# Moving 32 weight subtractions from VectorE to GpSimd in a two-layer diffusion trunk

## Chip, cores and metric

The kernel runs on one core of one Trainium2 chip. The metric is the device time of one execution in microseconds (us); the median of three runs stands for a kernel.

## What is computed

The reference passes 384 tokens (128 context tokens, 256 latent ones; model width 1024) through two layers. Each layer is a half-step SwiGLU FFN, a mixer of four head groups with one input and one output projection, and a second half-step FFN. Every sub-layer has an RMS norm, shift, scale and gate from a modulation vector, and a residual add. All data is fp32.

```
h = rms_norm(x, g) * (1 + scale) + shift
x = x + 0.5 * gate * ((silu(h @ wg) * (h @ wu)) @ wd)          # FFN, width 2816
x = x + gate * (concat(four mixers of (h @ w_in)) @ w_out)     # mixer
```

## The kernel before

Activations are kept transposed: x is eight tiles x[k] of 128 features by 384 tokens. Every large product is made of three fp32r matmuls (`mm3`, L203 to L207): a weight is split into a high part (a ScalarE copy to fp32r, L196) and a low part (weight minus high part, L197, on VectorE), an activation likewise, and high*high (L205), high*low (L206) and low*high (L207) are added up in PSUM. `weights` loads a piece of weights by a DMA of the SP queue into a "raw" buffer (5 of them) and splits it into a "hi" buffer (5) and a "lo" buffer (4). A lo buffer is free again when the matmuls that read it are done.

An FFN (`ffn`) runs over 22 blocks of 128 hidden features, in two halves of 11. A block f loads a gate piece (z = 0) and an up piece (z = 1), 128x1024 each, and makes 24 matmuls into a PSUM bank g and 24 into a bank u. The "d" banks are two, so g of block f+1 waits until g of block f has been read. The first four blocks ("early") work on x scaled but not yet normalised (hh and hl, L259 and L260, 386 columns) so that they can begin before the norm factor rstd is known. Their results are multiplied by rstd afterwards (g at L267, u at L312), and `hidden` (L287 to L290) makes the normalised inputs of the later blocks meanwhile. After each half come eight down blocks (dn).

The output projection (in `dense`, L477 to L490) runs in two passes (ph) over eight output blocks j; a pass adds four of the eight mixer tiles. Each block has a 128x512 piece of weights, twelve matmuls, and then `add_x` (L273), which reads the bank and updates x[j]. In the second pass, `nxt(j)` makes hh and hl of x[j] for the next FFN, and `ssq.add(j)` adds the squares of x[j]: for j = 1 to 6 this add is on GpSimd, for j = 7 on VectorE (L234). rstd is worked out from that sum, by a matmul with ones (L240) and two activations.

VectorE also makes part of the modulation vectors of later sub-layers between these (L170, "junk"). Which instructions an engine runs is written in the code; in which order each engine's queue holds them is settled when the kernel is built, by a scheduler that goes by program order, by when operands and buffers come free, and by its own durations. On the chip each engine's queue runs in order.

Of the kernel before, what the change touches and what calls it, by code (L numbers as in the profile page):

```python
# [11 lines left out]
ALU = mybir.AluOpType  # L12
# [4 lines left out]
D = 1024  # L17
# [26 lines left out]
def trunk(ctx, tc, a):  # L44
    nc = tc.nc
    V, S, G, PE = nc.vector, nc.scalar, nc.gpsimd, nc.tensor
# [7 lines left out]
    def nm(s):  # L54
        cnt[0] += 1
        return f"{s}_{cnt[0]}"


    def dbank(s):
        return ps.tile([P, 512], F32, tag="d", name=nm(s), bufs=2)  # L60
# [14 lines left out]
    def slot(grp, s, *shapes, dt=F32):  # L75

        t, o, out = sb.tile([P, WIDTH[grp]], dt, tag=grp, name=nm(s), bufs=NSLOT[grp]), 0, []
        for sh in shapes:
            n = int(np.prod(sh))
            v = t[:, o:o + n]  # L80
            if len(sh) == 2:
                v = v.rearrange("p (a b) -> p a b", a=sh[0])
            elif len(sh) == 3:
                v = v.rearrange("p (a b c) -> p a b c", a=sh[0], b=sh[1])
            out.append(v)
            o += n
        assert o <= WIDTH[grp], (s, o)
        return out if len(out) > 1 else out[0]

    def one(s, dt=F32):  # L90
        return sb.tile([P, T], dt, tag="one", name=nm(s), bufs=4)

    def tiny(grp, s, n):
        return sb.tile([P, 8], F32, tag="tiny" + grp, name=nm(s), bufs=7)[:, :n]
# [22 lines left out]
    def load_w(src, s):  # L117
        t = sb.tile([P, 1024], F32, tag="raw", name=nm("raw" + s), bufs=5)
        n = src.shape[-1]
        nc.sync.dma_start(out=t[:, :n], in_=src)  # L120
        return t[:, :n]
# [67 lines left out]
        return gt  # L189


    def split_w(raw, s):
        n = raw.shape[-1]
        hi = sb.tile([P, 1024], F32R, tag="hi", name=nm("hi" + s), bufs=5)[:, :n]
        lo = sb.tile([P, 1024], F32R, tag="lo", name=nm("lo" + s), bufs=4)[:, :n]
        S.activation(hi, raw, AF.Copy)  # L196
        V.tensor_tensor(lo, raw, hi, op=ALU.subtract)  # L197
        return hi, lo

    def weights(src, s):  # L200
        return split_w(load_w(src, s), s)

    def mm3(out, w, o, x, first, last):  # L203
        wh, wl = w[0][:, o:o + P], w[1][:, o:o + P]
        PE.matmul(out, wh, x[0], start=first, stop=False)  # L205
        PE.matmul(out, wh, x[1], start=False, stop=False)  # L206
        PE.matmul(out, wl, x[0], start=False, stop=last)  # L207

    def split_act(src, hi, lo):
        S.activation(hi, src, AF.Copy)  # L210
        V.tensor_tensor(lo, src, hi, op=ALU.subtract)
# [33 lines left out]
    def log_exp():  # L245
        tc.keep_in_program_order(S.preload_act_table_set(LOGEXP))
# [29 lines left out]
    def ffn(l, i, rstd, ab, nxt, side, hook=None):  # L276

        side = side()
        gt = None
        ssq = Sumsq(int(l == NL - 1 and i == 1))  # L280
        h = [None] * KD

        def hidden(k):
            t, xr = slot("M", "h", (2, T), dt=F32R), one("xr")
            at, bt = ab
            for g, cs in GROUPS:
                V.scalar_tensor_tensor(xr[:, cs], x[k][:, cs], at[:, k, g:g + 1], rstd[:, cs],  # L287
                                       op0=ALU.mult, op1=ALU.mult)
                S.activation(t[:, 0, cs], xr[:, cs], AF.Identity, bias=bt[:, k, g:g + 1])
                V.scalar_tensor_tensor(t[:, 1, cs], xr[:, cs], bt[:, k, g:g + 1], t[:, 0, cs],  # L290
                                       op0=ALU.add, op1=ALU.subtract)
            h[k] = (t[:, 0, :], t[:, 1, :])

        for half in range(2):
            act = []
            for fi in range(HF):
                f = half * HF + fi
                w = [weights(a["w_gu"][l, i, f, :, z * D:(z + 1) * D], "gu") for z in range(2)]
                bg, bu = dbank("g"), dbank("u")
                early = f < 4  # L300
                order = [(z, k) for z in range(2) for k in range(KD)]
                if f == 0:
                    order.sort(key=lambda zk: zk[1])
                for z, k in order:
                    mm3((bg, bu)[z][:, :NX if early else T], w[z], k * P,
                        (hh[:, k, :], hl[:, k, :]) if early else h[k], k == 0, k == KD - 1)
                g, u = one("g"), one("u")
                if early:
                    sh = tiny("s", "sh", 2)
                    normed(g, bg, rstd, AF.Silu)  # L310
                    V.tensor_copy(sh, bu[:, T:NX])
                    V.tensor_tensor(u, bu[:, :T], rstd, op=ALU.mult)  # L312
                    for q, cs in GROUPS:
                        V.scalar_tensor_tensor(u[:, cs], u[:, cs], sh[:, q:q + 1], g[:, cs], op0=ALU.add, op1=ALU.mult)
                    for k in range(f * KD // 4, (f + 1) * KD // 4):
                        hidden(k)
                else:
                    S.activation(g, bg[:, :T], AF.Silu)  # L318
                    V.tensor_tensor(u, g, bu[:, :T], op=ALU.mult)
                if fi % 2 == 0:  # L320
                    ah = slot("H", "ah", (2, T), dt=F32R)
                    al = slot("H", "al", (2, T), dt=F32R)
                act.append((ah[:, fi % 2, :], al[:, fi % 2, :]))
                split_act(u, *act[-1])
                if f == NF - 1:
                    log_exp()
                if hook and f == 2:
                    hook()
                side()
            if gt is None:  # L330
                gt = gate(l, 2 * i)
            for j in range(KD):
                b = dbank("dn")
                fi = 0
                for z, n in ((0, 6), (1, 5)):
                    src = a["w_dn"][l, i, half, j]
                    w = weights(src[:, :6 * P] if z == 0 else src[:, 6 * P:], "dn")
                    for o in range(n):
                        mm3(b[:, :T], w, o * P, act[fi], fi == 0, fi == HF - 1)
                        fi += 1  # L340
                add_x(j, b, gt)
                if half == 1:
                    nxt(j)
                    ssq.add(j)
                side()
        return ssq
# [71 lines left out]
    def mixers(l, rstd, gt, ab, nxt):  # L418
# [46 lines left out]
        def dense():  # L465
            for n, (name, c) in enumerate(HALVES):
                b = dbank("in")
                if (name, c) == KR:
                    narrow(b)
                else:  # L470
                    w = weights(a["w_in"][l, WIDE.index((name, c))], "in")
                    for k in range(KD):
                        mm3(b[:, :NX], w, k * P, (hh[:, k, :], hl[:, k, :]), k == 0, k == KD - 1)
                take[name](c, b)
                yield 4.0 if n < 6 else 1.5 if (name, c) == KR else 6.84
            done["in"] = True
            for ph, ks in enumerate(OUT_PARTS):  # L477
                for jj in range(4):
                    for z in range(2):
                        j = 2 * jj + z  # L480
                        w = weights(a["w_out"][l, ph, jj, :, z * 512:(z + 1) * 512], "out")
                        b = dbank("out")
                        for n, k in enumerate(ks):
                            yield from wait(("mix", k))
                            mm3(b[:, :T], w, n * P, mix[k], n == 0, n == 3)
                        add_x(j, b, gt)
                        if ph == 1:
                            nxt(j)
                            ssq.add(j)
                        yield 2.6  # L490
# [486 lines left out]
    def side(units):  # L977

        places = [[] for _ in range(NF + 2 * KD)]
        for by, l, n, p0, p1 in units:  # L980
            g = (ada_pe if by == "PE" else ada_dve)(l, n)
            for k in range(KD):
                places[p0 + k * (p1 + 1 - p0) // KD].append(g)
            if by == "PE":
                places[p1 + 1].append(g)
        first = min([NF] + [u[3] for u in units if u[0] == "DVE"])
        places[max(first - 2, 0)].insert(0, requests_of())
        todo = iter(places)

        def f():  # L990
            for g in next(todo):
                next(g)
        return f
# [179 lines left out]
```

## Time and profile before

| what | value |
|---|---|
| median of 3 runs (lowest to highest) | 1554.87 us (1551.93 to 1558.4) |
| the profiled execution's own time | 1555.26 us |
| its span, first to last instruction | 1553.5 us |
| TensorE busy, share of the span | 1510.0 us, 97% |
| VectorE busy | 1177.9 us, 76% |
| ScalarE busy | 749.1 us, 48% |
| GpSimd busy | 99.1 us, 6% |
| granted TensorE clock, mean | 0.998 |

Shares are means over stages with different limits: TensorE is nearly always busy, VectorE has stretches in which it is full and others in which it waits. In rows of the trace, DVE is VectorE, ACT is ScalarE, POOL is GpSimd, PE is TensorE, and L260 is line 260 of the kernel.

### The profile page before, as it was taken

What the parts mean: (1) busy time and instruction counts of PE and PEld (TensorE: products, weight loads), DVE (VectorE), ACT (ScalarE), POOL (GpSimd) and SP (SyncE); (2) the same over time, 40 slices, a digit from 0 to 9 for tenths busy, and PEclk for the clock granted to TensorE, in tenths of its full rate; (3) what the DMA queues carried; (4) which work ended last, traced back from release to release, by engine and by line L of the source; (5) the groups of instructions that cost most, each with busy time, mean ns of one, the idle gap of its engine ahead of it and who ended that gap; (6) DMA issues with size and microseconds to landing.
All of it is one profiled execution on the core that took longest, in us unless ns stands there. A gap on an engine that the chain in (4) does not pass through costs nothing.

```text
span 1553.5 us, 26681 instructions
## 1 busy us (share of the span) xinstructions
PE 1510.0 (97%) x10108; PEld 1422.1 (92%) x10108; DVE 1177.9 (76%) x2649; ACT 749.1 (48%) x1330; POOL 99.1 (6%) x122
## 2 busy tenths in 40 slices
PE   6999999999999999999999999999999999999997
PEld 2999999998778999999999999999877799999997
DVE  3879998969956997997987799786797599544433
ACT  4632233457788743233454323345677874333332
POOL 1000000100130100000000000001014010000001
PEclk9999999999999999999999999999999999999999
DMA  9776775652133555765654577555211145544331
GB/s 346 252 235 206 242 236 201 190 183 83 36 94 119 160 190 183 244 230 175 203 175 150 177 233 236 183 172 173 85 65 46 66 154 182 159 143 140 120 102 60
DMA packets 84464, 257.31 MB, mean 166 GB/s; under 512 B 11120, under 2 KB 14416, under 8 KB 84080
## 3 DMA queue, kind: packets, MB, share of 16 engines
q1 hardware_dynamic: 83184, 254.14, 49.9%
q8 instruction: 79, 1.29, 0.3%
q0 software_dynamic: 1152, 1.48, 0.3%
q14 instruction: 49, 0.40, 0.1%
HBM read 252.53 MB, written 2.26 MB: 164 GB/s over the span
## 4 chain that ended last, share of the span: by engine, by line
PE 66%; DVE 19%; DMA 8%; issue 4%; ACT 3%; SPq 0%; DVEq 0%; ACTq 0%
DVE junk L170 6%; PE u L205 6%; PE u L207 6%; PE u L206 6%; PE g L205 6%; PE g L207 6%; PE g L206 6%; PE dn L206 5%; PE dn L205 5%; PE dn L207 5%; DMA rawada<-in_w_adaT 4%; DVE logu L197 3%; PE in L206 3%; PE in L207 3%; PE in L205 3%
## 5 line engine op out<-in xcount | busy, mean ns | idle before, releaser
L170 DVE SCALAR_TENSOR_TENSOR junk<-rawada,req 128x512 f32<-128x512 f32 x480 | 339.1, 706 | 40.0 <-DMA rawada<-in_w_adaT 30.2
L196 ACT ACTIVATE higu<-rawgu 128x1024 fp32r<-128x1024 f32 x176 | 186.2, 1060 | 295.6 <-DMA rawgu<-in_w_gu 91.2
L197 DVE TENSOR_TENSOR logu<-rawgu,higu 128x1024 fp32r<-128x1024 f32 x176 | 214.5, 1222 | 35.6 <-PE g L207 19.8
L205 PE MATMUL dn<-ah,hidn 128*128 128x384 f32 x704 | 236.8, 336 | 0.0
L207 PE MATMUL dn<-ah,lodn 128*128 128x384 f32 x704 | 236.6, 336 | 0.0
L206 PE MATMUL dn<-al,hidn 128*128 128x384 f32 x704 | 236.6, 336 | 0.0
L196 ACT ACTIVATE hidn<-rawdn 128x768 fp32r<-128x768 f32 (+1 forms) x128 | 101.5, 793 | 254.5 <-PE dn L206 71.7
L205 PE MATMUL u<-h,higu 128*128 128x384 f32 x576 | 194.0, 337 | 3.1 <-DVE x L273 2.5
L205 PE MATMUL g<-h,higu 128*128 128x384 f32 x576 | 194.4, 338 | 1.8 <-ACT g L318 1.6
L206 PE MATMUL g<-h,higu 128*128 128x384 f32 x576 | 193.7, 336 | 0.0
L207 PE MATMUL u<-h,logu 128*128 128x384 f32 x576 | 193.6, 336 | 0.0
L207 PE MATMUL g<-h,logu 128*128 128x384 f32 x576 | 193.6, 336 | 0.0
L206 PE MATMUL u<-h,higu 128*128 128x384 f32 x576 | 193.6, 336 | 0.0
L197 DVE TENSOR_TENSOR lodn<-rawdn,hidn 128x768 fp32r<-128x768 f32 (+1 forms) x128 | 113.2, 885 | 30.1 <-issue 17.0
L205 PEld LDWEIGHTS dn<-ah,hidn 128*128 128x128 f32 x704 | 132.3, 188 | 0.4 <-issue 0.3
L206 PEld LDWEIGHTS dn<-al,hidn 128*128 128x128 f32 x704 | 132.4, 188 | 0.0
L207 PEld LDWEIGHTS dn<-ah,lodn 128*128 128x128 f32 x704 | 132.3, 188 | 0.0
L234 POOL TENSOR_TENSOR ssq<-ssq,sq 128x384 f32<-128x384 f32 x42 | 46.9, 1117 | 1160.5 <-DVE hl L260 752.7
L205 PEld LDWEIGHTS g<-h,higu 128*128 128x128 f32 x576 | 108.3, 188 | 5.0 <-ACT g L318 2.4
L205 PEld LDWEIGHTS u<-h,higu 128*128 128x128 f32 x576 | 108.3, 188 | 4.3 <-issue 3.1
L206 PEld LDWEIGHTS g<-h,higu 128*128 128x128 f32 x576 | 108.3, 188 | 0.2 <-DVE h L290 0.2
L206 PEld LDWEIGHTS u<-h,higu 128*128 128x128 f32 x576 | 108.3, 188 | 0.0
(297 smaller groups left out, 2844.9 us busy)
## 6 DMA issues: line engine op xcount, KB each, us to landing
rawgu<-in_w_gu SPq DMA_DIRECT2D x176, 512.0 KB, 4.2
rawada<-in_w_adaT SPq DMA_DIRECT2D x120, 512.0 KB, 3.7
rawdn<-in_w_dn SPq DMA_DIRECT2D x64, 384.0 KB, 3.3
rawdn<-in_w_dn SPq DMA_DIRECT2D x64, 320.0 KB, 3.0
rawin<-in_w_in SPq DMA_DIRECT2D x38, 512.0 KB, 3.7
rawada<-in_w_ada SPq DMA_DIRECT2D x24, 512.0 KB, 6.2
rawout<-in_w_out SPq DMA_DIRECT2D x32, 256.0 KB, 2.7
req<-in_c SPq DMA_DIRECT2D x16, 256.0 KB, 4.0
```

Of the source, the lines that this page charges most:

```text
L170: V.scalar_tensor_tensor(xbank("junk")[:, 0, :], t[:, z * 512:(z + 1) * 512], 1.0, requests[v, z], op0=ALU.mult, op1=ALU.mult, accum_out=s ...
L196: S.activation(hi, raw, AF.Copy)
L197: V.tensor_tensor(lo, raw, hi, op=ALU.subtract)
L205: PE.matmul(out, wh, x[0], start=first, stop=False)
L206: PE.matmul(out, wh, x[1], start=False, stop=False)
L207: PE.matmul(out, wl, x[0], start=False, stop=last)
L234: (V if self.n == KD - 1 else G).tensor_tensor(self.acc, self.acc, sq, op=ALU.add)
```

## The change

`split_w` and `weights` get an argument `low`, the engine of the subtraction at L197. It is GpSimd (G) for the up piece of blocks 0 to 3 of each FFN (4 pieces of 128x1024 in each of 4 FFNs, 16 in all) and for all pieces of the output projection's second pass (8 pieces of 128x512 in each of 2 layers, 16 in all). The other low parts stay on VectorE.

```diff
-    def split_w(raw, s):
+    def split_w(raw, s, low=None):
...
         S.activation(hi, raw, AF.Copy)
-        V.tensor_tensor(lo, raw, hi, op=ALU.subtract)
+        (low or V).tensor_tensor(lo, raw, hi, op=ALU.subtract)
         return hi, lo
-    def weights(src, s):
-        return split_w(load_w(src, s), s)
+    def weights(src, s, low=None):
+        return split_w(load_w(src, s), s, low)
...
-                w = [weights(a["w_gu"][l, i, f, :, z * D:(z + 1) * D], "gu") for z in range(2)]
+                w = [weights(a["w_gu"][l, i, f, :, z * D:(z + 1) * D], "gu", G if f < 4 and z == 1 else None)
+                     for z in range(2)]
...
-                        w = weights(a["w_out"][l, ph, jj, :, z * 512:(z + 1) * 512], "out")
+                        w = weights(a["w_out"][l, ph, jj, :, z * 512:(z + 1) * 512], "out", G if ph == 1 else None)
```

## Rows read from the trace of the kernel before

**Rows 1.** The page's first part: busy us (share of span) xinstructions per engine.

```profile
PE 1510.0 (97%) x10108; PEld 1422.1 (92%) x10108; DVE 1177.9 (76%) x2649; ACT 749.1 (48%) x1330; POOL 99.1 (6%) x122
```

**Rows 2.** Waits of PE, whole span: us in total, times, longest us.

```profile
PE ada L145 <- DMA rawada<-in_w_ada: 13.3, 15, 5.6
...
PE u L205 <- ACT hh L259: 1.4, 1, 1.4
...
PE g L205 <- DVE g L267: 1.1, 3, 0.5
...
PE u L205 <- ACT higu L196: 0.4, 1, 0.4
```

**Rows 3.** Timeline of PE, 508 to 528 us: start, us, instruction, [idle before <-releaser].

```profile
510.13 0.34 PE L207 MATMUL out<-mix,loout 128*128 128x384 f32 x1
510.78 0.41 PE L205 MATMUL out<-mix,hiout 128*128 128x384 f32 x1 [0.31 <-ACT hh L259]
...
514.00 0.41 PE L205 MATMUL g<-hh,higu 128*128 128x386 f32 x1 [0.88 <-ACT hh L259]
...
517.20 0.42 PE L205 MATMUL u<-hh,higu 128*128 128x386 f32 x1 [0.49 <-DVE x L273]
...
524.40 0.41 PE L205 MATMUL g<-hh,higu 128*128 128x386 f32 x1 [0.29 <-DVE g L267]
```

**Rows 4.** Timeline of DVE, 495 to 580 us.

```profile
499.29 0.74 DVE L260 SCALAR_TENSOR_TENSOR hl<-x,A,hh 128x128 fp32r<-128x128 f32 x2
...
504.27 0.74 DVE L273 SCALAR_TENSOR_TENSOR x<-out,G,x 128x128 f32<-128x128 f32 x2
...
507.00 1.55 DVE L197 TENSOR_TENSOR logu<-rawgu,higu 128x1024 fp32r<-128x1024 f32 x1
508.48 1.50 DVE L260 SCALAR_TENSOR_TENSOR hl<-x,A,hh 128x128 fp32r<-128x128 f32 x2
...
518.77 0.54 DVE L234 TENSOR_TENSOR ssq<-ssq,sq 128x384 f32<-128x384 f32 x1
```

**Rows 5.** Timeline of POOL, whole span.

```profile
19.66 1.00 POOL L234 TENSOR_TENSOR ssq<-ssq,sq 128x384 f32<-128x384 f32 x1 [19.21 <-ACT sq L232]
...
429.49 0.86 POOL L889 TENSOR_TENSOR d<-dh 128x406 f32<-128x406 f32 x1 [7.51 <-DVE sc L383]
...
504.03 1.05 POOL L234 TENSOR_TENSOR ssq<-ssq,sq 128x384 f32<-128x384 f32 x1 [1.04 <-ACT sq L232]
...
508.53 1.18 POOL L234 TENSOR_TENSOR ssq<-ssq,sq 128x384 f32<-128x384 f32 x1 [1.05 <-ACT sq L232]
```

**Rows 6.** DVE groups by form, 498.03 to 519.31 us: xcount | busy us, mean ns.

```profile
L260 DVE SCALAR_TENSOR_TENSOR hl<-x,A,hh 128x256 fp32r<-128x256 f32 x8 | 6.1, 764 | 0.0
L197 DVE TENSOR_TENSOR logu<-rawgu,higu 128x1024 fp32r<-128x1024 f32 x4 | 5.2, 1294 | 0.0
...
L197 DVE TENSOR_TENSOR loout<-rawout,hiout 128x512 fp32r<-128x512 f32 x4 | 2.8, 688 | 0.0
L260 DVE SCALAR_TENSOR_TENSOR hl<-x,A,hh 128x128 fp32r<-128x128 f32 x8 | 2.7, 341 | 0.0
```

**Rows 7.** Three stretches: length; busy us of PE, PEld, DVE, ACT, POOL; clock, DMA, GB/s.

```profile
498.03:519.31 21.28, 19.59 (x110) 18.72 (x109) 21.01 (x42) 17.76 (x33) 6.63 (x6) 1.00 0.62 200
788.97:797.43 8.46, 7.09 (x41) 6.80 (x40) 8.46 (x14) 4.65 (x8) 1.17 (x1) 1.00 0.76 237
524.16:549.87 25.71, 25.47 (x144) 25.50 (x145) 25.59 (x63) 15.84 (x31) 0.00 (x0) 1.00 0.42 134
```

**Rows 8.** Timeline of DVE, 780 to 812 us.

```profile
794.45 0.73 DVE L273 SCALAR_TENSOR_TENSOR x<-dn,G,x 128x128 f32<-128x128 f32 x2
...
803.15 0.16 DVE L266 COPY sh<-g 128x2 f32<-128x2 f32 x1 [5.71 <-PE g L207]
```

**Rows 9.** DVE and PE in the timeline, 529 to 533 us.

```profile
529.87 0.55 DVE L267 TENSOR_TENSOR g<-g,rstd 128x384 f32<-128x384 f32 x1
...
532.98 0.34 PE L205 MATMUL g<-hh,higu 128*128 128x386 f32 x1
```

## The prediction

> **What bounds the kernel now.** I read the page's busy times first. TensorE is busy 1510.0 of 1553.5 us, 97% [rows 1]: work that is taken off another engine gives at most the time that TensorE now waits for that engine. So the second view is TensorE's waits. The largest item, 13.3 us for the first modulation weights, is a load at the start that the change does not touch [rows 2]. What it could touch stands in the third view, the timeline of TensorE at the end of the first mixer: it idles 0.31, 0.88 and 0.49 us while banks come free, and 0.29 us before the g matmuls of block 1 of the next FFN, whose bank waits for the normalisation at L267 [rows 3]. Together that is 2.0 us. Here VectorE is the reason: in the 21.28 us that end there it is busy 21.01 [rows 7].
>
> The fourth view, VectorE's timeline set beside GpSimd's, decides the case. A pair of L260 instructions takes 0.74 us when GpSimd rests, but the pair that begins at 508.48 takes 1.50 [rows 4]. GpSimd ran a 128x384 add from 508.53 to 509.71 [rows 5]. The pair ends at 508.48 + 1.50 = 509.98, 0.27 after the add: its second instruction stood until the add was over. The subtraction at 507.00 takes 1.55 in the same way. L273, however, takes its plain 0.74 from 504.27 to 505.01 [rows 4], wholly inside the GpSimd add of 504.03 to 505.08 [rows 5]. L260 and L197 read two tensors from SBUF, L273 reads one from PSUM and one from SBUF. I read this as: an instruction of VectorE with two SBUF inputs and a two-input instruction of GpSimd do not run at the same time; one with a PSUM input is free. It goes both ways, since the GpSimd add takes 1.00 undisturbed and 1.18 when it meets VectorE [rows 5].
>
> **A rule of the Trainium skill on this.** The page "SBUF — State Buffer", section "Who interferes with whom", says more than these rows: that the lock is held for the whole instruction, whatever its length. The rows agree for adds of 1.2 us; no run here shows a longer one. If GpSimd let VectorE in halfway through a longer one, the excess below would be about half; by the rule it is whole.
>
> From the rows alone, where the bar lasts to the end of the add, I take the whole duration.
>
> **The price of a subtraction on GpSimd.** No row shows a 128x1024 or 128x512 subtraction there, nor one that writes fp32r. The nearest rows are the two-tile add of 384 columns in 1.00 us, 2.6 ns a column, and an add of one tile with itself shifted, 406 columns in 0.86, 2.1 ns a column [rows 5]. That gives 2.17 to 2.67 us for 1024 columns and 1.08 to 1.33 for 512. I take 2.6 and 1.3, near the two-tile add, since the subtraction reads two tiles too. On VectorE the same work costs 1.21 (the mean of 1.294 over four, with the blocked one of 1.55 taken out: (4 x 1.294 - 1.55)/3) and 0.69 [rows 4, 6]. So each moved piece frees VectorE of 1.21 or 0.69 us and bars its two-input instructions for 2.6 or 1.3.
>
> The Trainium skill has another price: "GPSIMD Engine Reference", section 3.1, gives 4497 ns for an add of 2048 columns, from which I estimate 2.25 us for 1024 columns and 1.12 for 512. No run here shows it. The sum below would come to about 8 us by it instead of 11.
>
> **Mixer ends, twice (once per layer).** From 498.03 to 519.31 I add up all that excludes each other: L260 eight pairs of 0.74 = 5.9; L197 4 x 1.21 + 4 x 0.69 = 7.6; the last square sum on VectorE 0.5 [rows 4]; GpSimd's adds 6.63 [rows 7]. The sum is 20.6 of 21.28: about 0.7 free. The change takes out four out pieces and two up pieces (blocks 0 and 1), 4 x 0.69 + 2 x 1.21 = 5.2, and adds 4 x 1.3 + 2 x 2.6 = 10.4. The excess is 10.4 - 5.2 - 0.7 = 4.5 us; with the low prices 2.8 (4 x 1.08 + 2 x 2.17 = 8.7), with the high ones 4.8. The other four out pieces fall before 498, where lo buffers are ready several blocks ahead; I cost them at nothing, hidden by TensorE's matmuls. The 4.5 reaches TensorE nearly whole, as it already waits there for this very chain: L273 stands behind L260 in VectorE's queue, the banks behind L273, and L267 behind the square sum and rstd [rows 3]. GpSimd's adds for j = 1 to 6 queue behind the subtractions as well, and the last add behind them. Twice 4.5 is 9.0 us (5.6 to 9.6).
>
> **Start of layer 1's first FFN.** From 788.97 to 797.43 VectorE is busy throughout [rows 7], and TensorE waits 1.4 us for the u bank [rows 2], which the L273 of 794.45 frees [rows 8]. One up piece lies ahead of it: 2.6 - 1.21 = 1.4 us later (0 to 2.8, if the second lies ahead too). The square sum is not critical here: VectorE idles 5.71 us after it, waiting for TensorE [rows 8].
>
> **Start of the first FFN.** TensorE waits 0.4 us for the first up piece's high part [rows 2]; the low part comes 1.4 us later, and the matmuls of g can go ahead of it. I take 0.7 (0 to 1.4).
>
> **Blocks 1 to 3 of each FFN.** VectorE is busy 25.59 of 25.71 us [rows 7]. The two up pieces that are split here (blocks 2 and 3) put it back by 2 x 1.4 = 2.8 at most. L267 of block 1 is done at 530.42, its bank is wanted at 532.98 [rows 9], so 2.5 us are spare. At most 0.3 per FFN, 1.2 in all, is left; I take nothing. What covers it is this spare time and the one-SBUF-input instructions (L266, L267, L311, L312), which can run beside GpSimd.
>
> **Sum.** 9.0 + 1.4 + 0.7 = 11.1 us. On the profiled execution, 1555.26 (span 1553.5 and 1.8 around it), that is 1566.4; it lies 0.4 above the median of the runs, so I forecast 1566. The likeliest case's own range is 5.6 to 9.6 + 2.8 + 1.4 + 1.2 = 15 us more, 1560.5 to 1570.
>
> **Rivals.** (1) *Hidden.* The subtractions fall where VectorE runs L273 or waits, and little reaches TensorE: 0 to 4 us, 1555 to 1559. For it: in the tail L273 takes eight times 0.74 [rows 4], 6 us, in which GpSimd may work freely, and the queue orders are made anew. Against: 0.7 us free in 21.28. (2) *The relief pays.* This is the other side: VectorE's chain gets shorter by 5.2 us in each mixer end, and the bank waits go. It decides if VectorE is barred by a GpSimd subtraction for less than the 1.21 or 0.69 us that it is freed of. The gain is at most the waits: twice 2.0 at the mixer ends [rows 3], 1.4 at layer 1 and 0.4 at the start [rows 2], 5.8 us, so 1549. With the restart that each wait brings (0.65 us from one start to the next at 510.13 where the gap reads 0.31 [rows 3]) perhaps 8, 1547. Against: [rows 4, 5] show the bar whole. (3) *All of it serial.* Each of the 32 pieces puts VectorE's chain back by the full difference, and GpSimd's queue holds the square sums back on top: 16 x 1.4 + 16 x 0.6 = 32 us, 1587. Against: spare time outside the tails, 5.71 us at one place [rows 8].
>
> **How the numbers follow.** The likeliest case gets 0.55, hidden 0.28, relief 0.10, serial 0.07. About 0.5%, 7.8 us, is what a measurement of this kernel can tell from no change: slower means over 1562.6, faster under 1547.1. Of the likeliest case I put 0.07 below that bound (low prices, nothing at the FFN starts), so slower is 0.48 + 0.07 = 0.55; relief reaches beyond 1547.1 in half of its cases, 0.05; the same is 0.40. The range is 1554 to 1574: it takes in the hidden case and the likeliest one's with some of the serial, and leaves out relief and the rest.
>
> **What would show it.** In the new profile: 16 subtractions of 128x1024 on POOL at 2.2 to 2.7 us and 16 of 128x512 at 1.1 to 1.35; L260 pairs between 498 and 520 well over 0.74; the gaps before the g and u matmuls at the mixer ends longer, 4 us each time in all; the stretch to L267 of block 1 longer; nothing changed from block 4 on and inside the mixers. The prediction is wrong if L260 and L197 keep their times beside a POOL subtraction, if POOL's price is under 1.3 us for 1024 columns, or if the new queue order puts L273 ahead of the barred instructions.

## The result and the profile after

| | before | after |
|---|---|---|
| median of the runs, us | 1556.51 (1551.93 to 1558.4, 4 runs) | 1579.01 (1577.55 to 1579.46, 4 runs) |
| profiled execution, us | 1555.26 | 1579.02 |
| its span, us | 1553.5 | 1577.2 |

The ratio is 1.0147, 95% interval 1.013 to 1.0163: 22.5 us slower by the medians. The direction was forecast, the size was not: 1566 with a range to 1574.

The page of the changed kernel, busy times by engine, against [rows 1]:

```profile
PE 1517.1 (96%) x10108; PEld 1423.9 (90%) x10108; DVE 1185.9 (75%) x2617; ACT 748.0 (47%) x1330; POOL 161.3 (10%) x154
```

GpSimd has 62.2 us more. VectorE was relieved of 32 instructions and is 8.0 us *busier*: what it kept takes longer. The changed kernel's groups on POOL (busy us, mean ns) give the price of the moved pieces:

```profile
L197 POOL TENSOR_TENSOR logu<-rawgu,higu 128x1024 fp32r<-128x1024 f32 x16 | 41.2, 2574 | 73.6 <-ACT higu L196 47.2 <-ACT g L269 19.1 <-DMA c_invc<-in_invc 6.3
L197 POOL TENSOR_TENSOR loout<-rawout,hiout 128x512 fp32r<-128x512 f32 x16 | 21.1, 1318 | 14.1 <-PE out L207 8.3 <-ACT qa L416 5.8
```

These are 2.57 and 1.32 us, where the prediction took 2.6 and 1.3. Now the end of layer 0's mixer: first VectorE's timeline of the changed kernel, then GpSimd's, then the pair of 511.52 with its two halves kept apart, then TensorE's two long waits and three windows around the second (length; busy PE, PEld, DVE, ACT, POOL; clock, DMA, GB/s).

```profile
509.38 0.74 DVE L273 SCALAR_TENSOR_TENSOR x<-out,G,x 128x128 f32<-128x128 f32 x2
510.03 1.57 DVE L197 TENSOR_TENSOR logu<-rawgu,higu 128x1024 fp32r<-128x1024 f32 x1
511.52 3.68 DVE L260 SCALAR_TENSOR_TENSOR hl<-x,A,hh 128x128 fp32r<-128x128 f32 x2
515.13 0.73 DVE L273 SCALAR_TENSOR_TENSOR x<-out,G,x 128x128 f32<-128x128 f32 x2
...
519.00 3.59 DVE L260 SCALAR_TENSOR_TENSOR hl<-x,A,hh 128x128 fp32r<-128x128 f32 x2
522.51 0.73 DVE L273 SCALAR_TENSOR_TENSOR x<-out,G,x 128x128 f32<-128x128 f32 x2
523.16 0.68 DVE L170 SCALAR_TENSOR_TENSOR junk<-rawada,req 128x512 f32<-128x512 f32 x1
```

```profile
511.55 1.02 POOL L234 TENSOR_TENSOR ssq<-ssq,sq 128x384 f32<-128x384 f32 x1 [1.03 <-ACT sq L232]
512.52 2.40 POOL L197 TENSOR_TENSOR logu<-rawgu,higu 128x1024 fp32r<-128x1024 f32 x1
...
518.48 2.82 POOL L197 TENSOR_TENSOR logu<-rawgu,higu 128x1024 fp32r<-128x1024 f32 x1 [0.49 <-ACT hh L259]
521.27 1.03 POOL L234 TENSOR_TENSOR ssq<-ssq,sq 128x384 f32<-128x384 f32 x1
```

```profile
L260 DVE SCALAR_TENSOR_TENSOR hl<-x,A,hh 128x256 fp32r<-128x256 f32 x1 | 2.6, 2560 | 0.0
...
L260 DVE SCALAR_TENSOR_TENSOR hl<-x,A,hh 128x128 fp32r<-128x128 f32 x1 | 1.2, 1197 | 0.0
```

```profile
516.00 0.42 PE L205 MATMUL out<-mix,hiout 128*128 128x384 f32 x1 [3.06 <-ACT hh L259]
523.38 0.42 PE L205 MATMUL u<-hh,higu 128*128 128x386 f32 x1 [3.27 <-ACT hh L259]
```

```profile
519.00:523.00 4.00, 1.11 (x7) 0.79 (x5) 4.00 (x5) 0.94 (x2) 3.30 (x2) 1.00 0.53 190
523.00:527.00 4.00, 3.62 (x13) 3.18 (x13) 3.93 (x11) 2.48 (x4) 0.00 (x0) 0.68 0.19 72
527.00:531.00 4.00, 4.00 (x21) 3.86 (x20) 0.23 (x2) 3.57 (x4) 0.00 (x0) 0.89 0.46 131
```

The L260 pair that took 0.74 us before [rows 4] begins at 511.52 beside two GpSimd instructions that follow each other without a gap, 511.55 to 514.92, and ends at 515.20: its first half (128 columns, 1.20 us) stood until the add was over, its second (256 columns, 2.56 us) until the subtraction was. Behind it in VectorE's queue is L273, which reads a bank; TensorE, which waits for that bank, stands 3.06 us instead of 0.31 [rows 3] (the list names L259, which had long been done). The same comes again at 519.00. After a stretch in which TensorE was busy 1.11 of 4.00 us, its granted clock is 0.68 of full speed in the next 4 us and 0.89 in the 4 after those; before, it was 1.00 in the stretch at this place [rows 7].

A second loss comes later, in blocks 1 to 4 of the same FFN. VectorE's timeline of the changed kernel, GpSimd's two subtractions there, and TensorE's:

```profile
533.18 2.44 DVE L287 SCALAR_TENSOR_TENSOR xr<-x,A,rstd 128x128 f32<-128x128 f32 x1
...
542.63 2.72 DVE L170 SCALAR_TENSOR_TENSOR junk<-rawada,req 128x512 f32<-128x512 f32 x1
...
562.44 0.55 DVE L313 TENSOR_TENSOR u<-u,rstd 128x384 f32<-128x384 f32 x1
...
565.97 1.14 DVE L290 SCALAR_TENSOR_TENSOR h<-xr,mod,h 128x256 fp32r<-128x256 f32 x3
```

```profile
533.07 2.40 POOL L197 TENSOR_TENSOR logu<-rawgu,higu 128x1024 fp32r<-128x1024 f32 x1 [10.76 <-ACT higu L196]
541.86 2.92 POOL L197 TENSOR_TENSOR logu<-rawgu,higu 128x1024 fp32r<-128x1024 f32 x1 [6.39 <-ACT g L269]
```

```profile
563.14 0.41 PE L205 MATMUL u<-h,higu 128*128 128x384 f32 x1 [0.66 <-DVE u L313]
...
565.91 0.69 PE L205 MATMUL g<-h,higu 128*128 128x384 f32 x1 [1.84 <-ACT h L289]
566.40 0.52 PE L206 MATMUL u<-h,higu 128*128 128x384 f32 x1
566.72 0.52 PE L207 MATMUL u<-h,logu 128*128 128x384 f32 x1
```

An L287 of 0.34 us takes 2.44, a side instruction (L170) of 0.70 takes 2.72, each until a GpSimd subtraction is over. Some 20 us later block 4 stands 0.66 and 1.84 us, first for the normalised u (L313, L312 before), then for the last of the normalised inputs that `hidden` makes (L287 to L290). Then its matmuls start 0.32 us apart, where 0.17 is usual: the granted clock is 0.57 from 565 to 569, which costs another 1.7 us (4.00 x 0.43).

To see where the time went, I took the start of the same matmul in two traces and let the difference grow from stage to stage. The first column of numbers is the changed kernel against the one before; the others belong to the experiments, e6 against the kernel before and the rest each a pair named in its head (all us).

| stage, and the start in the trace before of the matmul that ends it | change | e6 | e8 - e7 | e10 - e9 | e12 - e13 | e15 - e16 |
|---|---|---|---|---|---|---|
| to block 1 of the first FFN, 46.26 | +0.2 | -1.7 | -1.0 | +2.0 | +2.1 | +3.0 |
| to the output projection, 484.52 | +2.0 | +2.1 | -0.2 | +0.7 | +1.4 | +3.4 |
| mixer end, layer 0, to block 1 of the next FFN, 524.40 | +6.3 | +7.2 | +3.0 | +4.2 | +4.5 | +4.5 |
| blocks 1 to 8 of that FFN, 587.45 | +5.0 | +3.1 | +5.6 | +0.1 | +4.1 | 0.0 |
| to layer 1, 792.73 | +1.0 | +0.7 | +0.6 | 0.0 | -0.2 | +1.2 |
| block 0 of layer 1's first FFN, 803.92 | +2.0 | +4.5 | +1.4 | +0.9 | +1.7 | +1.7 |
| to the output projection, 1225.96 | -0.4 | -1.0 | +0.6 | 0.0 | +0.2 | +0.1 |
| mixer end, layer 1, to block 1, 1274.63 | +4.4 | +7.3 | +4.4 | +4.1 | +4.9 | +4.0 |
| blocks 1 to 8 of that FFN, 1338.08 | +3.3 | +2.9 | +2.5 | -0.1 | +2.1 | 0.0 |

The change loses 10.7 us at the two mixer ends, 8.3 in blocks 1 to 8 of the two second FFNs (at block 4, as the rows show), 2.0 at layer 1's start. The two layers differ by 1.9 us at the mixer ends and by 1.7 in blocks 1 to 8. TensorE's granted clock accounts for both. In layer 0 it fell after the stall in each of these stages, which cost 4.00 x 0.32 + 4.00 x 0.11 = 1.7 us at the mixer end and 1.7 at block 4. In layer 1 it stayed at 1.00, though TensorE stood 3.06 and 3.14 us at that mixer end too. These two waits, then windows of the changed kernel, at block 4 in layer 0, behind the mixer end of layer 1 and over its blocks 1 to 8:

```profile
1279.99 0.41 PE L205 MATMUL out<-mix,hiout 128*128 128x384 f32 x1 [3.06 <-ACT hh L259]
...
1287.40 0.41 PE L205 MATMUL u<-hh,higu 128*128 128x386 f32 x1 [3.14 <-ACT hh L259]
```

```profile
565.00:569.00 4.00, 3.09 (x10) 3.09 (x11) 3.64 (x8) 1.55 (x5) 0.00 (x0) 0.57 0.47 176
1288.00:1292.00 4.00, 4.00 (x22) 3.73 (x22) 3.90 (x11) 3.37 (x5) 0.00 (x0) 1.00 0.17 66
1295.12:1361.83 66.71, 64.12 (x360) 62.77 (x361) 59.84 (x130) 30.05 (x52) 5.33 (x2) 1.00 0.51 173
```

Without the fall of the clock, blocks 1 to 8 lose 3.3 us in either layer. The first two stages move by up to 1.6 us each between kernels whose code there does not differ (against before, e13: -1.4 and -0.3; e16: -1.6 and -1.5), so I read no cause into them.

### The profile page after: what moved, and what is told of

Read it like the earlier page. It is cut to its first block, busy times and chain, and to the rows that moved or that the text cites. A ratio compares the mean times of both kernels' runs of the same rounds, so it can differ in the third digit from the quotient of the medians.

```text
span 1577.2 us, 26723 instructions
## 1 busy us (share of the span) xinstructions
PE 1517.1 (96%) x10108; PEld 1423.9 (90%) x10108; DVE 1185.9 (75%) x2617; ACT 748.0 (47%) x1330; POOL 161.3 (10%) x154
## 4 chain that ended last, share of the span: by engine, by line
PE 62%; DVE 21%; DMA 9%; issue 4%; ACT 4%; SPq 0%; POOL 0%; DVEq 0%; ACTq 0%
PE u L207 6%; DVE junk L170 6%; PE u L205 6%; DMA rawada<-in_w_adaT 6%; PE u L206 6%; PE g L206 5%; PE g L205 5%; PE g L207 5%; PE dn L206 4%; PE dn L205 4%; PE dn L207 4%; PE in L206 3%; PE in L207 3%; PE in L205 3%; DVE logu L197 2%
## 5 line engine op out<-in xcount | busy, mean ns | idle before, releaser
L170 DVE SCALAR_TENSOR_TENSOR junk<-rawada,req 128x512 f32<-128x512 f32 x480 | 343.5, 716 | 41.5 <-DMA rawada<-in_w_adaT 32.1
L197 DVE TENSOR_TENSOR logu<-rawgu,higu 128x1024 fp32r<-128x1024 f32 x160 | 196.1, 1227 | 38.5 <-PE g L207 22.9
L197 DVE TENSOR_TENSOR lodn<-rawdn,hidn 128x768 fp32r<-128x768 f32 (+1 forms) x128 | 113.3, 885 | 29.9 <-issue 17.0
```

The costliest lines, as they stand in the source:

```text
L170: V.scalar_tensor_tensor(xbank("junk")[:, 0, :], t[:, z * 512:(z + 1) * 512], 1.0, requests[v, z], op0=ALU.mult, op1=ALU.mult, accum_out=s ...
L197: (low or V).tensor_tensor(lo, raw, hi, op=ALU.subtract)
```

## Experiments

The theory after the result: **the bar**, as in the prediction (a VectorE instruction with two SBUF inputs and a GpSimd instruction with two do not run together), acting in the early blocks as well, where VectorE is too full to make up for it. Against it stood: **late low parts** (TensorE waits for pieces that GpSimd has not finished), **the queue** (the square-sum adds and the subtractions hold one another back on GpSimd), and **the order** (the scheduler made other queue orders, and these cost the time). Ratios are to the kernel before, timed beside it on the same chip.

### One half each: e1 and e2

e1 keeps only the output projection's pieces on GpSimd, e2 only the up pieces:

```diff
-   ... "gu", G if f < 4 and z == 1 else None)     # e1: None
-   ... "out", G if ph == 1 else None)             # e2: None
```

> Only the second-pass pieces of the output projection are subtracted on GpSimd; all up pieces stay on VectorE. Theory 1, the bar (a two-SBUF-input instruction of VectorE and a GpSimd instruction that reads SBUF exclude each other): per mixer end four pieces at 1.32 in place of 0.69 us, less 0.7 us that was free, is 1.8 us; twice that, 3 to 4 us over before, all of it between the second pass and block 1 of the next FFN, nothing elsewhere. Theory 2, lateness (the low parts come too late for TensorE): no change, since lo buffers are ready several blocks ahead. Theory 3, order (the scheduler fills the time that it holds to be free on VectorE with side work that then stands in front of urgent instructions): some change also in blocks 1 to 4 of the FFN after the mixer.

> Only the up pieces of blocks 0 to 3 are subtracted on GpSimd; the output projection's stay on VectorE. Bar: the rest of the 22.5 us, 17 to 20 us over before: at each mixer end 2 x (2.57 - 1.21) less 0.7, some 2 to 4 us, layer 1's first FFN 2 us, and all that was lost at blocks 2 to 5 of the FFNs (10 us). Lateness: the wait would be shown as u matmuls waiting for L197 on POOL. Order: the loss at block 4 stays even where no POOL instruction runs beside it, with side work (L170) standing ahead of L312 and L313.

e1 took 1558.49 us against 1555.98, ratio 1.0016 (1.0005 to 1.0027): 2.5 us, a little under the 3 to 4 expected. e2 took 1576.34, 1.0134 (1.0113 to 1.0155): 20.4 us. The halves add up to 22.9, the whole change cost 22.5. Sixteen short pieces cost an eighth of what sixteen long ones do, so the loss does not follow GpSimd's busy time (21 against 41 us) alone.

### GpSimd's work without the dependence: e5 and e6

In both, VectorE makes every low part as before, so no low part waits for GpSimd and VectorE is not relieved. GpSimd writes the raw buffer once nobody needs it any more: in e5 it only writes, in e6 it reads two tiles.

```diff
-        (low or V).tensor_tensor(lo, raw, hi, op=ALU.subtract)
+        V.tensor_tensor(lo, raw, hi, op=ALU.subtract)
+        if low is not None:
+            low.memset(raw, 0.0)                                  # e5, twice
+            low.tensor_tensor(raw, raw, hi, op=ALU.subtract)      # e6, once
```

> VectorE makes all low parts as before; behind each of the 32, GpSimd sets the raw buffer, which nobody reads any more, to zero twice (about 2.1 us for an up piece, 1.1 for an out piece), which writes SBUF and reads nothing. Bar by reads only: VectorE's instructions keep their times (an L260 pair 0.74 beside a memset), the kernel is within 4 us of before, what it loses being square sums that queue behind memsets. Bar by any GpSimd instruction: as in the run with unread subtractions, 20 us or more. Lateness: no change, the low parts are VectorE's.

> VectorE makes all low parts as before; behind each of the 32, GpSimd makes the same subtraction once more into the raw buffer, which nobody reads any more. No low part is later than before and VectorE is relieved of nothing. Bar: 25 to 45 us over before, since at each mixer end 4 x 1.32 + 2 x 2.57 less 0.7 free = 9.7 us come on top and the early blocks are barred 2.57 us per piece. Lateness: no change beyond 2 us. Order: no change beyond 3 us, as VectorE's queue holds what it held before.

e5: 1557.44, ratio 0.9998 (0.9977 to 1.0019). e6: 1582.68, 1.0174 (1.0153 to 1.0195), 26.7 us. VectorE's and GpSimd's timelines of e5 (L263 is its L260):

```profile
502.94 0.73 DVE L263 SCALAR_TENSOR_TENSOR hl<-x,A,hh 128x128 fp32r<-128x128 f32 x2
...
503.08 0.53 POOL L199 MEMSET rawout<- 128x512 f32 x1
```

and of e6 (its L262), at a 128x512 subtraction:

```profile
499.72 1.79 DVE L262 SCALAR_TENSOR_TENSOR hl<-x,A,hh 128x128 fp32r<-128x128 f32 x2
...
499.88 1.35 POOL L199 TENSOR_TENSOR rawout<-rawout,hiout 128x512 f32<-128x512 f32 x1 [0.79 <-DVE loout L197]
```

The same pair takes 0.73 beside a GpSimd instruction that only writes and 1.79 beside one that reads. The Trainium skill says the same in "SBUF — State Buffer", section "Who interferes with whom": a VectorE instruction with two SBUF inputs contends with a GpSimd instruction that reads SBUF and not with one that only writes it. By that rule e5 costs nothing and e6 the bar, and the runs agree: e5 is not told from no change (1.5 us by the medians), e6 loses 26.7.

Late low parts are ruled out: in e6 none waits for GpSimd, and it loses more than the change; and TensorE's waits in the changed kernel name no L197 either. The queue theory loses ground too, for in e5 the adds stand behind memsets on GpSimd at the mixer end, and by the starts of the same matmuls the two ends lose 0.0 and -0.4 us against before:

```profile
512.13 0.95 POOL L199 MEMSET rawgu<- 128x1024 f32 x1
513.13 0.95 POOL L200 MEMSET rawgu<- 128x1024 f32 x1
514.16 1.02 POOL L237 TENSOR_TENSOR ssq<-ssq,sq 128x384 f32<-128x384 f32 x1
```

The memsets hold GpSimd for 47.4 us in all, the subtractions of e6 for 64.0.

### Which blocks: e3 and e4

Only up pieces on GpSimd, in e3 those of blocks 0 and 1, in e4 those of blocks 2 and 3:

```diff
-   ... G if f < 4 and z == 1 else None)
+   ... G if f < 2 and z == 1 else None)           # e3
+   ... G if f in (2, 3) and z == 1 else None)     # e4
```

> Only the up pieces of blocks 0 and 1 are subtracted on GpSimd. Bar alone: these are the ones that run beside the L260 chain at the end of the sub-layer before; 3 us at each of the two mixer ends, 2 us at layer 1's first FFN, 1 us at the start: 8 to 10 us over before, and nothing lost at blocks 2 to 5. If the losses at blocks 2 to 5 come with the pieces of blocks 0 and 1 already, they are a consequence of the late start, not of the later pieces.

> Only the up pieces of blocks 2 and 3 are subtracted on GpSimd, when the mixer's end is past. The prediction's step for blocks 1 to 3: at most 0.3 us per FFN, 1.2 in all. Bar with VectorE full of side work: 3 to 5 us in each second FFN and 1 to 2 in each first, 8 to 12 in all, lost before blocks 1 to 5.

e3: 1568.25 against 1555.81, 1.008 (1.0062 to 1.0098), 12.4 us where 8 to 10 were expected. e4: 1564.81, 1.0062 (1.004 to 1.0083), 9.0 us. By the starts of the same matmuls e3 loses 4.2 and 3.9 us at the mixer ends and 2.0 at layer 1's start, 10.1 in all, and the rest spread over other stages; e4 loses nothing at the mixer ends and 5.2 and 4.9 in blocks 1 to 8 of the second FFNs. Blocks 2 and 3, whose pieces the prediction costed at nothing, cost 9 us by themselves.

### Is it full VectorE? e9 and e10, e12 and e13, e15 and e16

Three pairs, each of the kernel before and the changed one with the same edit. In e9 (before) and e10 (after) seven of eight steps of VectorE's side work are left out, so the modulation vectors are not the reference's:

```diff
-            t = load_w(a["w_adaT"][l, n, k], "ada")
-            for v in range(2):
+            if k == 0:
+                V.memset(sums, 0.0)
+            for v in range(2 if k == KD - 1 else 0):
+                t = load_w(a["w_adaT"][l, n, k], "ada")
```

> The kernel before, but of the side work on VectorE only every eighth step is computed (the loads and L170 for k below 7 are left out, so the modulation vectors are not the reference's). It is the base for its twin. Since VectorE has far less to do, it should be at or a little under before: 1540 to 1556 us.

> The changed kernel with the same seven eighths of the side work left out. Bar together with a full VectorE: at the mixer ends there is no side work, so about 9 to 11 us over its base stay, 2 us at layer 1's first FFN too, but the 10 us of blocks 1 to 5 shrink to under 3: 11 to 15 us over its base. If the loss at blocks 1 to 5 does not need a full VectorE: 20 to 23 us over its base.

e9 took 1545.93, e10 1556.09: the change costs 10.2 us without this side work (11 to 15 expected) and 22.5 with it. Blocks 1 to 8 lose nothing (the table's e10 - e9), the mixer ends 4.2 and 4.1. But leaving the work out also empties VectorE elsewhere and changes the queues. So the next pairs keep all work and only move it: the side work of the second FFNs starts at block 4 (e12 after, e13 before) or 6 (e15 after, e16 before).

```diff
-    [("DVE", 0, 8, 2, 10), ...        [("DVE", 1, 8, 1, 9)]]
+    [("DVE", 0, 8, 4, 10), ...        [("DVE", 1, 8, 4, 10)]]      # e12, e13
+    [("DVE", 0, 8, 6, 10), ...        [("DVE", 1, 8, 6, 10)]]      # e15, e16
```

> The changed kernel with all its work, but the side work of each layer's second FFN begins at block 4 and is due by block 10 (before: from block 2, or 1, to 10 or 9). In the instruction order this takes two to six L170 instructions out of the mixers' ends and four out of blocks 0 and 1. If VectorE's side work is what turns the bar into the stalls of blocks 1 to 5, these stalls (some 5 us in layer 0 and 3 in layer 1) go, about 1 us more at each mixer end with them, and the kernel stands 10 to 14 us over its own base, the unchanged kernel with the same shift: about 1566 to 1570 us if that base stays at 1556. If the stalls come from the new order of the weights' pieces, and leaving out the side work hid that by emptying VectorE everywhere, it stays 18 us or more over its base, about 1575. If side work packed into blocks 4 to 10 fills VectorE there, both kernels lose, and new waits for gate and hidden parts appear from block 6 on.

> The kernel before with the same later side work: the base of the run on the changed kernel. Blocks 0 to 3 have no stall there worth naming, so I expect 1553 to 1557 us: a gain of 1 to 2 us at most at the two mixer ends, where an L170 instruction stands between the bank reads. If blocks 4 to 10 become too full for VectorE it is slower than the kernel before by some us.

e12: 1572.49, ratio 1.0111 (1.0091 to 1.0132). e13: 1554.22, 0.9998 (0.9986 to 1.001). The difference of 18.3 us is what the order theory expected; mine expected 10 to 14. The loss in blocks 1 to 8 stayed, 4.1 and 2.1 us. VectorE's queue shows why that decides nothing: six side instructions still stood in blocks 2 and 3, four of them in one row ahead of the normalisation of block 2's u. The start at block 6 leaves none in blocks 0 to 3:

> The changed kernel with all its work; the side work of each layer's second FFN begins at block 6. Blocks 0 to 3 of these FFNs then hold no L170 instruction at all in VectorE's queue (with the start at block 4 still six in blocks 2 and 3). If full VectorE in the early blocks is what keeps the delay of the two barred L287 alive until block 4, it is made up by block 2 or 3 (the normalisation of u waits for TensorE again), block 4 waits for no hidden part, TensorE's clock stays at 1.00 there, and this kernel stands 10 to 13 us over its base. If the order of the weights' pieces makes these stalls, they stay, 17 us or more over the base.

> The kernel before with the same start at block 6, the base of the run on the changed kernel. 1551 to 1556 us if blocks 6 to 10 have room for four to eight L170 instructions each; some us slower than the kernel before if they have not, or if the gate of the first half comes late.

e15: 1570.79, 1.0106 (1.009 to 1.0121). e16: 1557.46, 1.0014 (1.0001 to 1.0027). The difference is 13.3 us, a little above the 10 to 13 of full VectorE and well under the order's 17; and the loss in blocks 1 to 8 is 0.0 in both layers. VectorE's timeline of e15:

```profile
532.53 2.45 DVE L287 SCALAR_TENSOR_TENSOR xr<-x,A,rstd 128x128 f32<-128x128 f32 x1
...
541.74 1.99 DVE L287 SCALAR_TENSOR_TENSOR xr<-x,A,rstd 128x128 f32<-128x128 f32 x1
...
549.47 0.16 DVE L312 COPY sh<-u 128x2 f32<-128x2 f32 x1 [0.57 <-PE u L207]
```

Two instructions are barred as in the changed kernel, 2.45 and 1.99 us, but at block 2 VectorE waits 0.57 us for TensorE again: the delay is made up. The windows show the room it has, first the changed kernel's over 20 us from the end of the first bar on and the 18 after that, then e15's over the 20 us that hold both bars:

```profile
536.00:556.00 20.00, 19.84 (x111) 19.18 (x111) 19.90 (x48) 10.01 (x20) 2.92 (x1) 1.00 0.43 151
556.00:574.00 18.00, 15.50 (x80) 14.79 (x79) 16.41 (x38) 8.79 (x17) 0.00 (x0) 0.91 0.45 154
```

```profile
528.00:548.00 20.00, 19.72 (x112) 19.43 (x111) 16.54 (x35) 13.01 (x23) 4.81 (x2) 1.00 0.30 106
```

VectorE is busy 19.90 of 20.00 us there in the changed kernel, 16.54 in e15. The changed kernel holds the same test within itself, since the first FFN of layer 1 has no side work before block 8. Its VectorE timeline:

```profile
820.77 2.48 DVE L287 SCALAR_TENSOR_TENSOR xr<-x,A,rstd 128x128 f32<-128x128 f32 x1
...
830.01 1.99 DVE L287 SCALAR_TENSOR_TENSOR xr<-x,A,rstd 128x128 f32<-128x128 f32 x1
...
837.75 0.16 DVE L312 COPY sh<-u 128x2 f32<-128x2 f32 x1 [0.57 <-PE u L207]
```

The same two bars, the same recovery, and by the table no loss behind block 1 of that FFN.

### The adds on GpSimd: e7, e8, e11

All square-sum adds on VectorE, in the kernel before (e7) and in the changed one (e8); in e11 only the mixers' adds, in the kernel before:

```diff
-                    (V if self.n == KD - 1 else G).tensor_tensor(self.acc, self.acc, sq, op=ALU.add)
+                    V.tensor_tensor(self.acc, self.acc, sq, op=ALU.add)
```

> The kernel before with all its square-sum adds on VectorE, so that GpSimd reads no SBUF at the ends of the sub-layers. Bar: at a mixer end an add that bars a chain that is full for about 0.76 us (the L260 pair of 1.50 instead of 0.74) is replaced by 0.47 on VectorE, three times per mixer end: 1 us less per mixer end, and the side work in the down blocks is barred no more: 0 to 4 us under before. If the bar does not matter: VectorE has 42 x 0.47 = 20 us more to do, at most 2 us over before.

> The changed kernel with all square-sum adds on VectorE: the subtractions no longer share GpSimd's queue with the adds. If the queue of GpSimd (an add late behind a subtraction) made part of the loss at the mixer ends: 4 us or more under the changed kernel. If only the bar did: GpSimd reads 42 x 1.1 us less, 1 to 4 us under it, still 18 us or more over before.

> The kernel before with only the mixers' square-sum adds on VectorE (12 of 42). Bar: the gain is at the mixer ends alone, 1 us each, 1 to 3 us under before. If the bar does not matter: within 1 us of before or over it.

e7: 1552.4, ratio 0.9984 (0.9975 to 0.9993). e11: 1553.36, 0.9989 (0.998 to 0.9998). e8: 1568.79 against 1554.97, 1.0092 (1.0078 to 1.0106): 13.8 us over the kernel before. But the kernel that differs from e8 by the change alone is e7. Against that, the change costs 16.4 us, and 22.5 with the adds on GpSimd.

The stages put little of the difference of 6.1 down to the adds (the table's e8 - e7 against change). Layer 0's mixer end loses 3.0 instead of 6.3, but 1.7 of the 6.3 are the fall of the clock behind its stall; layer 1's mixer end loses 4.4 in both, layer 1's start 1.4 instead of 2.0. That leaves, as an estimate, 2 us for the adds; 3.4 lie in the first two stages, into which I read no cause. So the queue theory is not shown to make a main part of the loss. Blocks 1 to 8 lose 5.6 and 2.5, with no add near; e8's granted clock there is 0.98 in layer 0 and 1.00 in layer 1, so part of the 5.6 is the clock's. Whether the 2 us are fewer bars or shorter queues, e8 does not tell apart.

### A faster version: e14 and e17

The bar holds in the kernel before too [rows 4, 5], so the change was also run the other way round: no adds on GpSimd, and the later side work (from block 4 in e14, from block 6 in e17).

> The kernel before with both: later side work, and all square-sum adds on VectorE (alone 2.5 us faster than the kernel before). If the two are independent, 1550 to 1554 us. If VectorE's room at the mixer ends is what both use, no more than the better of the two.

> As the one before, with all square-sum adds on VectorE. With the start at block 4 this pair gave 1548.8 us; if what it gains lies at the mixer ends, 1547 to 1550 us here too.

e14: 1548.77 us against 1554.2, ratio 0.996 (0.9946 to 0.9974); e17: 1551.47, 0.9973 (0.9962 to 0.9985). e14 beats both kernels, the one before by 0.4% and the changed one, by the two ratios (0.996 / 1.0147), by 1.8%. e17 missed the 1547 to 1550 expected. By the starts of the same matmuls, e14 gains 1.3, 1.5 and 1.5 us against before at the two mixer ends and at layer 1's start, about what e7 gains there (1.2, 1.5, 1.5). That it gains more than its parts in all (e7 0.9984, e13 0.9998) was measured and not explained.

## Why the prediction was half right

**The bar: right.** The rows of 1.2 us adds carried over to 2.4 us subtractions whole (the second half of the pair of 511.52 takes 2.56 and ends 0.28 us after the subtraction), and e5 and e6 show it apart from all else.

**The price: right.** 2.57 and 1.32 us against 2.6 and 1.3. Undisturbed it is 2.40; the estimate of 2.25 from the Trainium skill ("GPSIMD Engine Reference", section 3.1) is low, and the measurement decides.

**Mixer ends: right but for the clock.** 4.5 us each were predicted; layer 1 lost 4.4, layer 0 6.3. The sum had no term for the granted clock, which in layer 0 was 0.68 and 0.89 over the 8 us from 523 on, 1.7 us, and in layer 1 stayed at 1.00. Up to the matmul that the second wait holds back (517.20 before, 523.38 after; 1267.26 and 1287.40 in layer 1) both layers lose 4.0 us of this stage. A side instruction of 0.68 us (523.16, and 1287.18 in layer 1) stands ahead of the last L260 in either layer, so it does not make the difference.

**Starts: right in kind.** Layer 1's first FFN lost 2.0 (1.4 predicted, 0 to 2.8), the first one 0.2 (0.7, 0 to 1.4).

**Blocks 1 to 3: the step that failed.** It said "at most 0.3 per FFN, 1.2 in all, is left; I take nothing". The second FFNs lost 5.0 and 3.3 (1.7 of the 5.0 by the clock), and e4 puts 9 us on these pieces alone. The sum of 11.1 fell short by 11.4, and 8.3 of it lie here. Three things in the step were wrong.

- The delay per piece. I took the difference, 2.6 - 1.21 = 1.4. The bars cost 2.44 - 0.34 = 2.1 and 2.72 - 0.70 = 2.0, and the relief was spent again: from L266 of block 0 to the last `hidden` part VectorE now makes five subtractions and eight side instructions, where it made seven and six. That stretch grew from 31.95 us (523.62 to 555.57) to 35.00 (532.11 to 567.11).
- The cover. I named L266, L267 and the two of u, which read PSUM. What stood under GpSimd's subtractions was L287 (x and rstd, both in SBUF) and L170 (two SBUF tiles).
- The chain. I measured the spare time at g's bank for block 1, 2.5 us. The chain that held TensorE longest is `hidden`'s (1.84 us, after 0.66 for u's bank): block 4 reads its parts, and the last of them was close to late already. VectorE's last L290 of the kernel before, and the u matmul of block 4 that was then running on TensorE without a wait:

```profile
554.39 1.18 DVE L290 SCALAR_TENSOR_TENSOR h<-xr,mod,h 128x256 fp32r<-128x256 f32 x3 [0.23 <-ACT h L289]
...
556.25 0.34 PE L205 MATMUL u<-h,higu 128*128 128x384 f32 x1
```

It was done 5.60 us after block 4's first matmul (549.97), in the changed kernel 7.97 after (559.14), and by then TensorE had run out of matmuls that do without it. With VectorE at 25.59 of 25.71 us [rows 7], a row that I had, a delay there does not shrink; I put the spare time of another chain against it.

**Rivals.** Hidden and relief fell with the result. "All serial" named a second ingredient, GpSimd's queue holding the adds; e5 and e8 against e7 leave it some 2 us at most. Its 1587 was too high because places with room pay nothing, as layer 1's first FFN shows.

**Open.** The 2.0 us up to the first output projection, and 6.4 in the same stages of e15 against e16, have no shown cause; 3.1 of the 6.4 are e16's profiled execution, which is early there by 1.6 and 1.5 us against before and lies 3.6 under the median of its kernel. The order is not needed for the size in blocks 1 to 8: e6, with other queues, no relief and a granted clock of 1.00 there, loses 3.1 and 2.9, the change without the clock 3.3 and 3.3; e4, at a clock of 0.98 in both layers, loses 5.2 and 4.9. In e12 and e15 the clock fell at layer 0's mixer end ahead of the last bank wait (0.50 from 514.8 to 521.6 and from 516.4 to 523.2), and that end lost 4.5; how much of it is the clock's is not shown. Why the clock fell after some of these stalls and not after others is not shown.

## To carry to other kernels

Moving an elementwise instruction from VectorE to GpSimd frees VectorE for its short time and bars VectorE's two-SBUF-input instructions for GpSimd's long one; count per piece which of VectorE's instructions will stand under it, and do not subtract the relief where a scheduler fills the gap with other work. A delay of 2 us on an engine that is full stays until the engine has room, so look for the consumer with the least spare time in the whole full stretch, not for the nearest one. Where GpSimd already reads beside a full VectorE, try the opposite move: here the square-sum adds were worth taking back.

## What was not expected of the hardware

Two GpSimd instructions in a row bar two VectorE instructions in a row: of the L260 pair of 511.52 one half stood for an add of 1.02 and the other for a subtraction of 2.40 us, 3.68 instead of 0.74 together. GpSimd is not spared either: the subtraction of 541.86 takes 2.92 instead of 2.40; an L170 of 0.69 us had begun 0.01 us before it. A stall of TensorE can cost more than itself, and need not: after 1.11 busy us in 4.00 (519 to 523), the granted clock was 0.68 over the next 4 us, between its levels of 1.2 and 2.4 GHz; after 0.86 busy us in 4.00 (1284 to 1288) it stayed at 1.00, the upper level. At block 4 it was 0.50, the lower one, from 565.9 to 568.7, where the matmuls start 0.32 us apart. GpSimd's memsets of 128x512, 0.53 us each, delayed nothing that these runs can measure (e5).
